# Attention scores on one core: four heads side by side in 64x32 PE tiles, with k read at a stride of 256 B

## Chip, core and metric

The kernel runs on one core of one Trainium2 chip. The metric is the device time of one launch in microseconds. Three runs of the kernel before took 211.76, 212.16 and 212.25 us, so the median is 212.16 us.

## What is computed

```python
def setup_inputs():
    batch, heads, seq, dim = 8, 8, 512, 64
    ...
def reference(q, k):
    scale = 1.0 / np.sqrt(q.shape[-1])
    return (np.einsum('bhqd,bhkd->bhqk', q, k) * scale).astype(np.float32)
```

There are 64 products, one for each batch and head. Each multiplies a 512x64 q by a transposed 512x64 k and gives a 512x512 float32 matrix. The inputs are 16.8 MB, the output is 67.1 MB.

## The kernel before

The kernel is written with a tile library: it declares pools of buffers and operations, and a scheduler orders the instructions of each engine and puts in the waits.

**Loading.** `load(b)` reads the whole q and k of a batch (8 heads) into `qf` and `kf`, 128 partitions by 8 heads by 4 rows of 64 floats (lines L49 and L50). Partition p holds rows 4p to 4p+3 of every head, so a head's piece in one partition is 4x64x4 B = 1 KB of contiguous memory. Batch 0 is loaded in four pieces of two heads each, the others in one piece of 1 MB for q and one for k. `raw_pool` has three buffers. Batches 0 and 1 are requested at the start, batch b+2 in the middle of batch b. All transfers, loads and stores, are issued by SP, in one queue.

**Per pair of heads** (`g`, four per batch) GpSimd casts the q and the k of two heads to bf16 (L81; ScalarE and VectorE do it for the first pair). TensorE transposes them in eight 128x128 steps into PSUM (`tq`, `tk`, L89). ScalarE copies `tq` to `qT` (L92). VectorE copies `tk` to `kT` (L93) and reorders on the way: it writes the elements with a stride of four, so that the columns of k lie in their natural order and the matmul can read them contiguously. After the transpose the first head of the pair lies on partitions 0 to 63 and the second on 64 to 127.

**Matmuls.** For each of the four row groups of q there is one matmul for each head (L101): 64 rows deep, 128 columns of weights (`qT`), 512 columns of k streamed. The tile position puts the two heads in the two row halves of the array. Two row groups fill one `ps` buffer of a head (128 x 1024 floats, two PSUM banks). There are three such buffers. `evacuate` scales a full `ps` buffer into the output tile `o`, alternately on ScalarE (L63) and VectorE (L65).

**Storing.** One store for each pair of heads (L108) moves the 2 MB tile `o`: in each partition two pieces of 8 KB, one per head. `out_pool` has seven buffers of 16 KB per partition.

Of the kernel before, what the change touches and what calls it, by code (L numbers as in the profile page):

```python
# [1 line left out]

# [5 lines left out]


@with_exitstack  # L10
def kernel(
    ctx: ExitStack,
    tc: tile.TileContext,
    q: bass.AP,
    k: bass.AP,
    out: bass.AP,
):


    nc = tc.nc  # L20
    B, H, S, D = q.shape
    scale = 1.0 / (D ** 0.5)
    P = 128
    J = S // P
    PAIRS = H // 2

    f32 = mybir.dt.float32
    bf16 = mybir.dt.bfloat16

    q_r = q.rearrange("b h (p j) d -> b p h (j d)", j=J)  # L30
    k_r = k.rearrange("b h (p j) d -> b p h (j d)", j=J)
    out_r = out.rearrange("b h (p j) k -> b p h (j k)", j=J)

    consts = ctx.enter_context(tc.tile_pool(name="consts", bufs=1))
    raw_pool = ctx.enter_context(tc.tile_pool(name="raw", bufs=3))
    bf_pool = ctx.enter_context(tc.tile_pool(name="bf", bufs=3))
    t_pool = ctx.enter_context(tc.tile_pool(name="t", bufs=3))
    out_pool = ctx.enter_context(tc.tile_pool(name="out", bufs=7))
    tpsum_pool = ctx.enter_context(tc.tile_pool(name="tpsum", bufs=1, space=bass.MemoryType.PSUM))
    psum_pool = ctx.enter_context(tc.tile_pool(name="psum", bufs=3, space=bass.MemoryType.PSUM))  # L40

    raws = {}

    def load(b):
        qf = raw_pool.tile([P, H, J * D], f32, name="qf")
        kf = raw_pool.tile([P, H, J * D], f32, name="kf")
        step = 2 if b == 0 else H
        for h in range(0, H, step):
            nc.sync.dma_start(out=qf[:, h:h + step, :], in_=q_r[b, :, h:h + step, :])  # L49
            nc.sync.dma_start(out=kf[:, h:h + step, :], in_=k_r[b, :, h:h + step, :])  # L50
        raws[b] = (qf, kf)

    load(0)
    identity = consts.tile([P, P], dtype=bf16)
    make_identity(nc, identity)
    load(1)

    n_evac = 0

    def evacuate(dst, src):  # L60
        nonlocal n_evac
        if n_evac % 2 == 0:
            nc.scalar.mul(out=dst, in_=src, mul=scale)  # L63
        else:
            nc.vector.tensor_scalar(out=dst, in0=src, scalar1=scale, scalar2=None,  # L65
                                    op0=mybir.AluOpType.mult)
        n_evac += 1

    for b in range(B):
        qf, kf = raws.pop(b)  # L70
        for g in range(PAIRS):
            if g == PAIRS // 2 and b + 2 < B:
                load(b + 2)
            qb = bf_pool.tile([P, J, 2, D], bf16, name="qb")
            kb = bf_pool.tile([P, J, 2, D], bf16, name="kb")
            first = b == 0 and g == 0
            for slab, dst, copy in (
                (qf, qb, nc.scalar.copy if first else nc.gpsimd.tensor_copy),
                (kf, kb, nc.vector.tensor_copy if first else nc.gpsimd.tensor_copy),
            ):  # L80
                copy(out=dst.rearrange("p j h d -> p h j d"),  # L81
                     in_=slab[:, 2 * g:2 * g + 2, :].rearrange("p h (j d) -> p h j d", j=J))
            qT = t_pool.tile([P, J, P], bf16, name="qT")
            kT = t_pool.tile([P, P, J], bf16, name="kT")
            tq = tpsum_pool.tile([P, J, P], bf16, name="tq")
            tk = tpsum_pool.tile([P, J, P], bf16, name="tk")
            for slab, tp in ((qb, tq), (kb, tk)):
                for j in range(J):
                    nc.tensor.transpose(out=tp[:, j, :],  # L89
                                        in_=slab[:, j].rearrange("p h d -> p (h d)"),  # L90
                                        identity=identity)
            nc.scalar.copy(out=qT, in_=tq)  # L92
            nc.vector.tensor_copy(out=kT.rearrange("d p j -> d j p"), in_=tk)  # L93

            o = out_pool.tile([P, 2, J * S], f32, name="o")
            for i in range(0, J, 2):
                pss = [psum_pool.tile([P, 2, S], f32, name="ps") for _ in range(2)]
                for u in range(2):
                    for h in range(2):
                        rows = slice(h * D, (h + 1) * D)  # L100
                        nc.tensor.matmul(out=pss[h][:, u, :], lhsT=qT[rows, i + u, :],  # L101
                                         rhs=kT[rows].rearrange("d p j -> d (p j)"),
                                         start=True, stop=True,
                                         tile_position=(h * D, 0))
                for h in range(2):
                    evacuate(o[:, h, i * S:(i + 2) * S],
                             pss[h].rearrange("p u k -> p (u k)"))
            nc.sync.dma_start(out=out_r[b, :, 2 * g:2 * g + 2, :], in_=o)  # L108


# [1 line left out]
_INS = ['q', 'k']  # L112
_OUTS = [((8, 8, 512, 512), 'float32')]


# [23 lines left out]
```

## Time and profile before

| | |
|---|---|
| median of three runs | 212.16 us |
| the profiled execution | 212.47 us |
| its span on the core | 210.7 us |
| PE matmul busy | 123.5 us (59%), 512 instructions |
| PE weight load busy | 40.5 us (19%), 512 instructions |
| VectorE / ScalarE / GpSimd busy | 115.3 / 84.7 / 36.9 us |
| moved by DMA | 83.99 MB, mean 399 GB/s |
| store of one `o`: issue to landing | 19.3 us, median |

The span is the time between the first and the last instruction on the core in one profiled execution; the 1.77 us beside it lie around it. The profile gives busy time for each engine, the share of the 16 DMA engines that was busy in each slice of the span, groups of equal instructions with their mean duration, and for every wait which instruction ended it. A transfer's "landing" is the moment at which its semaphore is complete. A store is issued as soon as its tile is full, and then stands in line behind the transfers issued before it.

### The profile page before, as it was taken

The numbers are of one execution on the slowest core, as the hardware profiler recorded it, in microseconds if no ns is written. First come the engines' busy times: TensorE is split into PE (matmuls) and PEld (weight loads), VectorE is DVE, ScalarE is ACT, GpSimd is POOL, SyncE is SP. The second block draws the span as 40 slices with busy tenths as digits, with TensorE's granted clock in tenths as the row PEclk, the third lists the DMA queues.
The fourth block names the chain that finished last, engine by engine and source line by source line (L and its number), as shares of the span: only waits on it lengthen the run. The fifth ranks groups of instructions, "written<-read, shape, count | busy, mean of one in ns | idle before, by whom it ended". The sixth has DMA issues, their size and how long they took to land.

```text
span 210.7 us, 1559 instructions
## 1 busy us (share of the span) xinstructions
PE 123.5 (59%) x512; PEld 40.5 (19%) x512; DVE 115.3 (55%) x97; ACT 84.7 (40%) x98; POOL 36.9 (18%) x68
## 2 busy tenths in 40 slices
PE   1899999897778743886148870587705877000000
PEld 0323222322232102221032210422104221000000
DVE  0699989688748940688307872178712797100000
ACT  4456666565536432446134460345503555000000
POOL 1625213300530006200070000800008000000000
DMA  6999999999999999999999999999999999999990
GB/s 185 335 357 411 428 403 425 429 426 394 401 428 425 426 382 413 428 425 423 376 425 429 426 412 386 426 431 428 398 400 426 428 428 426 428 426 428 431 409 37
DMA packets 25448, 83.99 MB, mean 399 GB/s; under 512 B 864, under 2 KB 17248, under 8 KB 17248
## 3 DMA queue, kind: packets, MB, share of 16 engines
q1 hardware_dynamic: 25440, 83.89, 99.1%
q8 instruction: 4, 0.07, 0.1%
q14 instruction: 4, 0.03, 0.0%
HBM read 16.78 MB, written 67.11 MB: 398 GB/s over the span
## 4 chain that ended last, share of the span: by engine, by line
DMA 50%; PE 8%; DVE 6%; ACT 1%; issue 0%; POOL 0%; DVEq 0%
DMA kf<-in_k_dram 50%; PE ps L101 6%; DVE kT L93 4%; DVE o L65 2%; PE tk L89 2%; ACT o L63 1%; POOL kb L81 0%; PE tq L89 0%; DVEq L65 0%
## 5 line engine op out<-in xcount | busy, mean ns | idle before, releaser
L101 PE MATMUL ps<-kT,qT 64*128 64x512 bf16 x256 | 90.1, 615 | 15.5 <-DVE o L65 5.9
L65 DVE TENSOR_SCALAR o<-ps 128x1024 f32<-128x1024 f32 x64 | 78.1, 1228 | 20.1 <-PE ps L101 18.7
L63 ACT ACTIVATE o<-ps 128x1024 f32<-128x1024 f32 x64 | 64.2, 1022 | 47.9 <-PE ps L101 47.8
L93 DVE COPY kT<-tk 128x512 bf16<-128x512 bf16 x32 | 41.3, 1291 | 39.7 <-PE tk L89 39.1
L89 PE MATMUL tq<-identity,qb 128*128 128x128 bf16 x128 | 21.6, 303 | 36.5 <-POOL qb L81 23.2
L81 POOL CAST qb<-qf 128x512 bf16<-128x512 f32 x31 | 18.2, 613 | 117.5 <-DMA qf<-in_q_dram 103.0
L92 ACT COPY qT<-tq 128x512 bf16<-128x512 bf16 x32 | 18.7, 585 | 43.5 <-PE tq L89 40.7
L101 PEld LDWEIGHTS <-qT 64*128 64x128 bf16 x256 | 16.2, 111 | 56.8 <-issue 55.9
L89 PEld LDWEIGHTS <-qb 128*128 128x128 bf16 x128 | 12.9, 131 | 56.3 <-POOL qb L81 29.6
L89 PE MATMUL tk<-identity,kb 128*128 128x128 bf16 x128 | 19.5, 307 | 3.0 <-DVE kT L93 2.5
L81 POOL CAST kb<-kf 128x512 bf16<-128x512 f32 x31 | 18.3, 613 | 7.9 <-DMA kf<-in_k_dram 3.7
L89 PEld LDWEIGHTS <-kb 128*128 128x128 bf16 x128 | 12.2, 134 | 24.0 <-issue 19.1
L81 DVE CAST kb<-kf 128x512 bf16<-128x512 f32 x1 | 0.4, 427 | 4.7 <-DMA kf<-in_k_dram 4.7
L81 ACT ACT_TABLE_LOAD x1 | 1.3, 1283 | 0.7 <-PEq L123 0.7
L81 ACT CAST qb<-qf 128x512 bf16<-128x512 f32 x1 | 0.6, 617 | 1.4 <-DMA qf<-in_q_dram 1.4
masks.py:199 POOL TENSOR_SCALAR_AFFINE_SELECT identity<-identity 128x128 bf16<-128x128 bf16 x1 | 0.3, 292 | 0.1
masks.py:197 POOL MEMSET identity<- 128x128 bf16 x1 | 0.2, 204 | 0.3 <-POOLq L123 0.3
L123 POOL MEMSET const-float32-0.0<- 128x1 f32 x1 | 0.1, 98 | 0.2 <-issue 0.2
L123 POOL MEMSET const-bfloat16-1.0<- 128x1 bf16 x1 | 0.1, 101 | 0.0
L123 POOL MEMSET const-uint8-127<- 128x1 uint8 x1 | 0.1, 101 | 0.0
L123 POOL MEMSET const-float32-1.0<- 128x1 f32 x1 | 0.1, 98 | 0.0
## 6 DMA issues: line engine op xcount, KB each, us to landing
out_dram<-o SPq DMA_DIRECT2D x32, 2048.0 KB, 19.3
qf<-in_q_dram SPq DMA_DIRECT2D x7, 1024.0 KB, 26.0
kf<-in_k_dram SPq DMA_DIRECT2D x7, 1024.0 KB, 27.5
qf<-in_q_dram SPq DMA_DIRECT2D x4, 256.0 KB, 4.3
kf<-in_k_dram SPq DMA_DIRECT2D x4, 256.0 KB, 4.6
```

The costliest lines, as they stand in the source:

```text
L63: nc.scalar.mul(out=dst, in_=src, mul=scale)
L65: nc.vector.tensor_scalar(out=dst, in0=src, scalar1=scale, scalar2=None, op0=mybir.AluOpType.mult)
L81: copy(out=dst.rearrange("p j h d -> p h j d"), in_=slab[:, 2 * g:2 * g + 2, :].rearrange("p h (j d) -> p h j d", j=J))
L89: nc.tensor.transpose(out=tp[:, j, :], in_=slab[:, j].rearrange("p h d -> p (h d)"), identity=identity)
L92: nc.scalar.copy(out=qT, in_=tq)
L93: nc.vector.tensor_copy(out=kT.rearrange("d p j -> d j p"), in_=tk)
L101: nc.tensor.matmul(out=pss[h][:, u, :], lhsT=qT[rows, i + u, :], rhs=kT[rows].rearrange("d p j -> d (p j)"), start=True, stop=True, tile_p ...
L123: nc = _bacc.Bacc("TRN2", target_bir_lowering=False, num_devices=1)
```

## The change

The tiling of heads and rows changes. Eight heads become 2 (`x`) times 4 (`g`), and 128 partitions become 4 heads (`g`) times 32 groups of rows (`m`), each with 16 consecutive rows (`j`, R = 16).

- A partition now holds 16 rows of one head: 4 KB contiguous for each load piece, two pieces (`x`) per partition. k is requested before q, and batch 0 comes whole like the others.
- GpSimd does all casts, in 128x1024 pieces, four per batch.
- The transposes take 128 partitions by 64 columns: 64 per batch (2 operands, 16 `j`, 2 `x`), 512 in all, in place of 256 of 128x128. `x` selects partitions 0 to 63 or 64 to 127 of the result. Eight `j` share one PSUM buffer `tp` (two buffers).
- `kT` is copied as it lies, with `j` outside and partitions inside. The order of the columns of k is restored by the matmul's read: for each head `g` it walks over `m` outside and `j` inside, and a step of `j` is 128 bf16 elements, 256 B.
- A matmul is 64 rows deep with 32 columns of weights (one head's 32 row groups at one `j`) and 512 streamed columns. Eight such tiles, 2 row halves by 4 column groups, cover the array. There are 1024 in place of 256.
- An output tile `o` holds one `x`, four heads and 8 consecutive rows in each partition: 16 KB contiguous in a partition and in memory. Each half batch has two such tiles and two stores of 2 MB. `out_pool` has six buffers instead of seven; `bf`, `t` two instead of three.

```diff
-    q_r = q.rearrange("b h (p j) d -> b p h (j d)", j=J)
-    k_r = k.rearrange("b h (p j) d -> b p h (j d)", j=J)
-    out_r = out.rearrange("b h (p j) k -> b p h (j k)", j=J)
+    q_r = q.rearrange("b (x g) (m j) d -> b (g m) x (j d)", x=2, j=R)
+    k_r = k.rearrange("b (x g) (m j) d -> b (g m) x (j d)", x=2, j=R)
+    out_r = out.rearrange("b (x g) (m j) k -> b x (g m) j k", x=2, j=R)
...
-        for h in range(0, H, step):
-            nc.sync.dma_start(out=qf[:, h:h + step, :], in_=q_r[b, :, h:h + step, :])
-            nc.sync.dma_start(out=kf[:, h:h + step, :], in_=k_r[b, :, h:h + step, :])
+        nc.sync.dma_start(out=kf, in_=k_r[b])
+        nc.sync.dma_start(out=qf, in_=q_r[b])
...
+        for x in range(2):
+            for slab, dst in ((kf, kb), (qf, qb)):
+                nc.gpsimd.tensor_copy(out=dst[:, x].rearrange("p j d -> p (j d)"), in_=slab[:, x])
...
+        for slab in (kb, qb):
+            for j0 in range(0, R, JB):
+                tp = tpsum_pool.tile([P, JB, P], bf16, name="tp")
+                for j in range(JB):
+                    for x in range(2):
+                        nc.tensor.transpose(out=tp[x * D:(x + 1) * D, j, :],
+                                            in_=slab[:, x, j0 + j, :], identity=identity)
+                if slab is kb:
+                    nc.vector.tensor_copy(out=kT[:, j0:j0 + JB, :], in_=tp)
+                else:
+                    nc.scalar.copy(out=qT[:, j0:j0 + JB, :], in_=tp)
...
+        kTg = kT.rearrange("d j (g m) -> d g m j", g=G)
+        for j0 in range(0, R, JB):
+            os = [out_pool.tile([P, JB, S], f32, name="o") for _ in range(2)]
+            for j in range(0, JB, 2):
                 pss = [psum_pool.tile([P, 2, S], f32, name="ps") for _ in range(2)]
                 for u in range(2):
-                    for h in range(2):
-                        rows = slice(h * D, (h + 1) * D)
-                        nc.tensor.matmul(out=pss[h][:, u, :], lhsT=qT[rows, i + u, :],
-                                         rhs=kT[rows].rearrange("d p j -> d (p j)"),
-                                         start=True, stop=True,
-                                         tile_position=(h * D, 0))
+                    for g in range(G):
+                        cols = slice(g * M, (g + 1) * M)
+                        for x in range(2):
+                            rows = slice(x * D, (x + 1) * D)
+                            nc.tensor.matmul(out=pss[x][cols, u, :],
+                                             lhsT=qT[rows, j0 + j + u, cols],
+                                             rhs=kTg[rows, g, :],
+                                             start=True, stop=True,
+                                             tile_position=(x * D, g * M))
+                for x in range(2):
+                    evacuate(os[x][:, j:j + 2, :], pss[x])
+            for x in range(2):
+                nc.sync.dma_start(out=out_r[b, x, :, j0:j0 + JB, :], in_=os[x])
+            if j0 == 0 and b + 2 < B:
+                load(b + 2)
```

The scheduler decides where the requests stand in SP's queue. In the program that it builds from the changed kernel, SP first issues the loads of batches 0, 1 and 2 and of batch 3's k, then the stores from the first one on; batch 3's q comes behind the sixth store.

More of the change, by code (lines that the diff above doesn't have):

```diff
@@ L23 @@
     P = 128
-    J = S // P
-    PAIRS = H // 2
+    G = H // 2
+    M = P // G
+    R = S // M
+    JB = 8
     f32 = mybir.dt.float32
     bf16 = mybir.dt.bfloat16
-    q_r = q.rearrange("b h (p j) d -> b p h (j d)", j=J)
-    k_r = k.rearrange("b h (p j) d -> b p h (j d)", j=J)
-    out_r = out.rearrange("b h (p j) k -> b p h (j k)", j=J)
+    q_r = q.rearrange("b (x g) (m j) d -> b (g m) x (j d)", x=2, j=R)
+    k_r = k.rearrange("b (x g) (m j) d -> b (g m) x (j d)", x=2, j=R)
+    out_r = out.rearrange("b (x g) (m j) k -> b x (g m) j k", x=2, j=R)
     consts = ctx.enter_context(tc.tile_pool(name="consts", bufs=1))
     raw_pool = ctx.enter_context(tc.tile_pool(name="raw", bufs=3))
[L36 to L39, printed above, removed]
+    bf_pool = ctx.enter_context(tc.tile_pool(name="bf", bufs=2))
+    t_pool = ctx.enter_context(tc.tile_pool(name="t", bufs=2))
+    out_pool = ctx.enter_context(tc.tile_pool(name="out", bufs=6))
+    tpsum_pool = ctx.enter_context(tc.tile_pool(name="tpsum", bufs=2, space=bass.MemoryType.PSUM))
     psum_pool = ctx.enter_context(tc.tile_pool(name="psum", bufs=3, space=bass.MemoryType.PSUM))
@@ L44, in load @@
     def load(b):
-        qf = raw_pool.tile([P, H, J * D], f32, name="qf")
-        kf = raw_pool.tile([P, H, J * D], f32, name="kf")
-        step = 2 if b == 0 else H
-        for h in range(0, H, step):
-            nc.sync.dma_start(out=qf[:, h:h + step, :], in_=q_r[b, :, h:h + step, :])
-            nc.sync.dma_start(out=kf[:, h:h + step, :], in_=k_r[b, :, h:h + step, :])
+        qf = raw_pool.tile([P, 2, R * D], f32, name="qf")
+        kf = raw_pool.tile([P, 2, R * D], f32, name="kf")
+        nc.sync.dma_start(out=kf, in_=k_r[b])
+        nc.sync.dma_start(out=qf, in_=q_r[b])
         raws[b] = (qf, kf)
@@ L70 @@
         qf, kf = raws.pop(b)
[L71 to L96, printed above, removed]
@@ new lines @@
+        qb = bf_pool.tile([P, 2, R, D], bf16, name="qb")
+        kb = bf_pool.tile([P, 2, R, D], bf16, name="kb")
+        for x in range(2):
+            for slab, dst in ((kf, kb), (qf, qb)):
+                nc.gpsimd.tensor_copy(out=dst[:, x].rearrange("p j d -> p (j d)"), in_=slab[:, x])
+        qT = t_pool.tile([P, R, P], bf16, name="qT")
+        kT = t_pool.tile([P, R, P], bf16, name="kT")
+        for slab in (kb, qb):
[9 more added lines that the diff above has]
+                    nc.scalar.copy(out=qT[:, j0:j0 + JB, :], in_=tp)
@@ L105 @@
[L105 to L108, printed above, removed]
+                    for g in range(G):
[7 more added lines that the diff above has]
+                                             tile_position=(x * D, g * M))
```

## The prediction

> **What bounds the kernel now.** I read the busy line first, then the DMA rows, then the tail, then the PE timeline.
>
> ```profile
> PE 123.5 (59%) x512; PEld 40.5 (19%) x512; DVE 115.3 (55%) x97; ACT 84.7 (40%) x98; POOL 36.9 (18%) x68
> DMA  6999999999999999999999999999999999999990
> ...
> q1 hardware_dynamic: 25440, 83.89, 99.1%
> q8 instruction: 4, 0.07, 0.1%
> ...
> DMA 50%; PE 8%; DVE 6%; ACT 1%; issue 0%; POOL 0%; DVEq 0%
> ```
>
> No engine is busy for over 59% of the span, while the DMA row is full from the second slice to the last but one. The kernel is bound by its transfers. The busy time in stretches says at what rate, and how it ends:
>
> ```profile
> 8.00:11.00 3.00, 3.00 (x14) 1.04 (x11) 2.58 (x3) 1.94 (x2) 1.84 (x3) 1.00 1.04 350
> ...
> 190.00:200.00 10.00, 0.00 (x0) 0.00 (x0) 0.00 (x0) 0.00 (x0) 0.00 (x0) 1.00 1.01 429
> ...
> 206.00:207.00 1.00, 0.00 (x0) 0.00 (x0) 0.00 (x0) 0.00 (x0) 0.00 (x0) 1.00 0.16 66
> 207.00:208.00 1.00, 0.00 (x0) 0.00 (x0) 0.00 (x0) 0.00 (x0) 0.00 (x0) 1.00 0.06 25
> 208.00:209.00 1.00, 0.00 (x0) 0.00 (x0) 0.00 (x0) 0.00 (x0) 0.00 (x0) 1.00 0.06 25
> ```
>
> The last two numbers are the DMA engines' share and GB/s. Before the first store (12.2 us) only loads run, in 1 KB pieces: 350 GB/s. From 180 us on only stores run, in 8 KB pieces: 426 to 429. After 206.2 us a share of 0.06, one engine of 16, works on until 209.4: it lags by 3.2 us. The q8 row names a candidate: four instruction fetches of 16 KB, which I take to be for PE, whose 1026 rows of the program at 64 B would make 66 KB.
>
> The stores take 67.1 MB / 427.5 = 157.0 us. The transfers run from 1.9 to 206.2 us, so 47.3 us are left for 16.8 MB of loads: 355 GB/s, as the load-only stretch shows. The span is then 1.9 + 47.3 + 157.0 + 3.2 (lag) + 1.3 (from 209.4 to the end) = 210.7.
>
> The timeline gives PE's rates. Two matmuls of different row halves take 0.61 us together, two pairs 1.03:
>
> ```profile
> 45.06 0.61 PE L101 MATMUL ps<-kT,qT 64*128 64x512 bf16 x2 [0.42 <-DVE kT L93]
> ```
> ```profile
> 45.06 1.03 PE L101 MATMUL ps<-kT,qT 64*128 64x512 bf16 x4 [0.42 <-DVE kT L93]
> 46.03 0.61 PE L89 MATMUL tk<-identity,kb 128*128 128x128 bf16 x4
> ```
>
> A pass of 512 columns costs 0.42 us and about 0.19 us of latency once; a transpose costs (0.61 - 0.29) / 3 = 0.107 us.
>
> **What the Trainium skill says.** "TensorE: Matmul & The Clock Gate", Back-to-back issue gap, gives N / 1.2 ns for a cold array: 427 ns for 512 and 107 for 128 columns. The trace agrees with both, so the array runs at that rate although the granted clock is shown as 1.00. Its Part 3 reports small tiles in row and column groups running at once, 16 of them at 10.6 times one; the trace shows row halves together (0.61 above), no column groups. "SBUF — State Buffer", Door 1, says that an access needs two hits on a 16-byte line for full bandwidth. The new read of k hits every line once, with no such matmul in this trace. "DMA: Bandwidth & Descriptors", iDMA fabric, has a load stream of 4 KiB rows at 408.7 GB/s; the trace has only 1 KB loads.
>
> **The change part by part.**
>
> *Loads*, 4 KB pieces: 16.78 MB / 408.7 = 41.1 us, 6.2 less. A line through 1 KB at 355 and 8 KB at 427.5 GB/s gives 415 (40.4 us) as the better end; 47.3 is the worse. *Stores*, 16 KB pieces: I leave 157.0; that line gives 434 GB/s, so 2.4 us less is the better end, and a loss by the new 32 KB pitch of the partitions in memory isn't excluded but has nothing for it.
>
> *Instruction fetch.* The built program has 3074 PE rows for 1026. Three times four fetches at 3.2 / 4 = 0.8 us (0.62, two 8 KB pieces at one engine's 26.7 GB/s, at the low end) is 9.6 (7.4) us on the lagging engine; I take 8.4, so 5.2 more.
>
> Sum before any idle DMA: 1.9 + 41.1 + 157.0 + 8.4 + 1.3 = **209.7**.
>
> *The start* decides how long DMA idles. Before, 256 KB pieces let the first store go at 12.2 us. Now k of batch 0 (1 MB) lands at 1.9 + 2.6 + 0.85 (what the first 256 KB load took beyond its transfer) = 5.3, q at 7.9. POOL casts in the order k0, q0, k1, q1, each twice the 613 ns of L81: ends 6.5, 9.1, 10.3, 11.5. k's transposes need both halves: from 10.3. A batch has 64 transposes; with half the columns each costs 0.107 if serial, 0.053 if two column halves run at once; I take 0.08. k's 32 end at 12.9, q's at 15.4. ACT's copy of qT's first half (1.1 us, twice the 585 ns of L92) ends by 15.5, DVE's copies of kT (1.2, the price of L65) earlier. Matmuls start at 15.6.
>
> *The matmuls.* The eight tiles do not run side by side as the words say: in the built program the scheduler puts all eight matmuls of one `ps` buffer together, four column groups, then the same four at the next row, all in one row half. One buffer is two passes; the next buffer, in the other half, can overlap one. The pass is the unknown. Its ends: 0.427 us, as contiguous; 1.71, if the four column groups, which read the same partitions, share one line a cycle. A faster array (0.213) would gain at most 2 us at the start. The nearest row is L93's copy, which writes 2-byte elements 8 B apart: 1291 ns, against 585 for the contiguous copy of the same size (L92). That is 2.2 times, and the skill's two hits say the same, so I take **0.854**.
>
> The first store needs four buffers of each half: three buffers, 14 transposes of the next batch, three buffers, 6 transposes, a buffer, 7 transposes, a buffer. From 15.6: three at one pass each plus one, to 19.0; 20.1; 23.5; 24.0; the seventh is full at 25.9 and evicted (1.02) at 26.95, the eighth follows at 29.4. First bytes leave at 28.05. The seven loads queued ahead (7.34 MB) end at 19.9. DMA idles **8.2 us**.
>
> *After that* a half batch costs 8 buffers of max(0.854, (2 x 0.854 + 0.19 + 1.25) / 3 = 1.05) us, for three buffers and an eviction, or 1.2 where transposes break the overlap, and 32 x 0.08: 12.2 us. Its two stores take 9.8, with loads 12.4. Until loads come between the stores (behind the sixth) two half batches are late by 2.4 us: **4** in round. Later production, about 23 to 24.6 us a batch, just keeps up with DMA's 24.7.
>
> *At nothing:* DVE's 41.3 us of kT copies become 16 of about 1.2; no gain, as DVE has 45% idle. POOL casts the same bytes under DMA. Batch 3's k load waits on SP for the third cast (10.3), with the stores behind it; none is due before 26. Six `o` buffers for seven still queue 12 MB, 29 us of stores; if production fell behind, that cover is gone.
>
> Span 209.7 + 8.2 + 4 = 221.9; about 1 us of fetches falls into idle time: 221. Beside the span lie 1.77 us, and the profiled execution was 0.31 above the median: **222.4**.
>
> **The rivals.**
>
> *A strided pass costs nothing* (0.427). For it: the array takes a column only every 0.83 ns, and may need no second hit. The same chain gives the first store at 22.75, first bytes 23.85, 4 us idle, then no more: 213.7, in time **214.5** (209 to 217). The fetches and the late start eat the gain of the loads.
>
> *Faster.* One mechanism, the larger pieces, decides if the lag doesn't grow: fetches spread over engines (3.2 stays), loads at 415, stores at 434, a free stride with paired transposes (2 us idle). 1.9 + 40.4 + 154.6 + 3.2 + 1.3 + 2 = 203.4, **204.9**. It turns when lag and idle time together grow by less than what the pieces save (6.2 to 9.3 us). Against it: one engine's tail is in the trace.
>
> *PE becomes the bound.* Four column groups share one line a cycle: pass 1.71, a batch 16 x 1.71 + 64 x 0.08 + 1 = 33.5 us, eight 268, plus 10.3 ahead and 13 for the last evictions and stores: 291, **293**. For it: the four reads hit the same partitions at once.
>
> **How the numbers follow.** Stride at twice: 0.38. Free stride: 0.30. Faster: 0.13. PE-bound: 0.17, and 0.02 for the rest. The likeliest alone covers 216 to 240 (transposes 0.053 to 0.107, production just behind DMA). The range 204.5 to 242 takes in all but the PE-bound case and the edges. A measurement here can tell about 0.3%. Faster 0.13; same 0.06, out of the free stride; slower 0.81.
>
> **What would show it.** Loads alone at 400 to 415 GB/s; DMA empty from about 20 to 28 us; 12 q8 fetches and a one-engine tail of some 8 us; two passes of a `ps` in about 1.9 us. Wrong if the DMA row stays full at the start, if one `ps` takes 1.0 us, or if PE is busy throughout and the DMA row has gaps in every batch.

## The result, and the profile after

The changed kernel takes 233.55 us (median of four runs, 233.04 to 234.31) against 211.97 us before in the same comparison: 1.102 times, with an interval of 1.0986 to 1.1054. The prediction had the sign, but 10.2 us of loss where there are 21.6. The profiled execution has a span of 231.7 us, 21.0 more than before.

The head of the page, its DMA queues and its chain of waits:

```profile
PE 191.9 (83%) x1536; PEld 45.9 (20%) x1536; DVE 88.6 (38%) x80; ACT 82.1 (35%) x81; POOL 33.1 (14%) x38
PE   0289999999998989898898988898998989989700
PEclk9995667796575555566555555557555555557555
DMA  6995494979989999999999999999999998909896
...
q1 hardware_dynamic: 8960, 83.89, 89.2%
q8 instruction: 12, 0.20, 0.3%
...
PE 77%; ACT 8%; DVE 5%; DMA 3%; POOL 1%; issue 1%; SPq 0%
PE ps L103 69%; PE tp L86 7%; ACT o L65 6%; DMA qf<-in_q_dram 3%; ACT qT L91 3%; DVE o L67 3%; DVE kT L89 2%; POOL qb L77 0%; POOL kb L77 0%; SPq L51 0%
```

The bound has moved. PE rose from 123.5 to 191.9 us of busy time, and the chain, half of which was DMA, now runs through PE for 77%, 69% in the matmuls. DMA has dips: at the start, then small ones, and one at 200 us (DMA share 0.38 from 200 to 210 us).

The groups of the matmul and of VectorE's copy of k, then the stretches of the start (busy times and numbers of instructions of PE, PEld, DVE, ACT and POOL, then clock, DMA share and GB/s):

```profile
L103 PE MATMUL ps<-kT,qT 64*32 64x512 bf16 x1024 | 161.3, 1026 | 15.5 <-ACT o L65 13.5
...
L89 DVE COPY kT<-tp 128x1024 bf16<-128x1024 bf16 x16 | 11.0, 686 | 16.4 <-PE tp L86 16.3
```
```profile
18.00:20.00 2.00, 2.00 (x33) 1.10 (x33) 0.00 (x0) 1.03 (x1) 1.44 (x3) 0.50 1.03 408
20.00:22.00 2.00, 2.00 (x16) 0.13 (x4) 1.13 (x1) 0.00 (x0) 0.81 (x1) 0.50 0.21 84
22.00:24.00 2.00, 2.00 (x18) 0.43 (x14) 1.46 (x3) 1.02 (x1) 0.00 (x0) 0.50 0.00 0
24.00:26.00 2.00, 2.00 (x19) 0.60 (x23) 0.46 (x1) 1.03 (x1) 0.00 (x0) 0.50 0.00 0
26.00:28.00 2.00, 2.00 (x24) 0.31 (x11) 0.76 (x1) 0.00 (x0) 0.00 (x0) 0.75 0.67 287
```

A single matmul takes 1026 ns where the kernel before had 615. DMA is all but empty from about 20.6 to 26.6 us: the loads queued ahead are done, and the first store is issued at 25.91.

The steady state is in the chain of waits. This is one full turn of it (start, duration, what; steps of "issue" below 0.05 us are left out):

```profile
123.71 9.85 PE ps L103 x62
133.59 1.03 ACT o L65
134.66 3.63 PE ps L103 x24
138.31 1.23 DVE o L67
139.54 0.60 DVE kT L89
140.15 0.70 DVE kT L89
140.90 1.08 PE tp L86 x16
142.00 1.02 ACT qT L91
143.06 6.66 PE ps L103 x39
149.74 1.03 ACT o L65
150.81 9.86 PE ps L103 x64
```

From 123.71 to 150.81 is 27.1 us, and the next batches repeat it (177.91, 205.00). The three matmul stretches hold 8, 3 and 5 `ps` buffers and take 9.85 + 3.63 + 6.66 = 20.1 us. Twice PE stands still while ScalarE evicts a buffer, 1.1 us each. Between 138.29 and 143.06 lie the transposes and the copies of `kT` and `qT`, 4.8 us.

DMA would need less for a batch: 2.1 MB of loads at 418 GB/s (the stretch from 8 to 12 us) and 8.4 MB of stores at 431 (e4 below) are 24.5 us. Little room is left, as its share over a turn (143.06 to 170.17 us) is 0.98. But PE waits for no transfer in that turn: its waits are 2.2 us for ScalarE's evictions, 0.5 for `qT` and 0.4 for `kT`. So DMA is fed too slowly by PE, and nothing that the larger transfers save is left.

At a standstill only one of the three `ps` buffers is full. These are the evictions that lead up to the first one:

```profile
130.57 1.03 ACT L65 ACTIVATE o<-ps 128x1024 f32<-128x1024 f32 x1 [0.75 <-PE ps L103]
131.81 1.23 DVE L67 TENSOR_SCALAR o<-ps 128x1024 f32<-128x1024 f32 x1 [1.50 <-PE ps L103]
133.59 1.02 ACT L65 ACTIVATE o<-ps 128x1024 f32<-128x1024 f32 x1 [1.98 <-PE ps L103]
134.66 3.60 PE L103 MATMUL ps<-kT,qT 64*32 64x512 bf16 x24 [1.12 <-ACT o L65]
```

Two buffers are free from 131.60 and 133.04 us on, yet PE waits for the third, which it has only just filled. At 149.72 us it is the same.

Not all batches take 27.1 us. The four that begin at 88.87, 115.97, 143.06 and 170.17 do. The three before them took 74.4 us, from the first matmul at 14.50 to 88.87, 24.8 us each on average. There the chain has transposes of the next batch between the matmul stretches, and only two standstills:

```profile
14.50 3.61 PE ps L103 x23
18.11 0.89 PE tp L86 x12
19.00 3.53 PE ps L103 x24
22.53 0.46 PE tp L86 x6
```

### The profile page after: what moved, and what is told of

It is laid out like the page before. It is cut to its first block, busy times and chain, and to the rows that moved or that the text cites. A ratio compares the mean times of both kernels' runs of the same rounds, so it can differ in the third digit from the quotient of the medians.

```text
span 231.7 us, 3444 instructions
## 1 busy us (share of the span) xinstructions
PE 191.9 (83%) x1536; PEld 45.9 (20%) x1536; DVE 88.6 (38%) x80; ACT 82.1 (35%) x81; POOL 33.1 (14%) x38
## 4 chain that ended last, share of the span: by engine, by line
PE 77%; ACT 8%; DVE 5%; DMA 3%; POOL 1%; issue 1%; SPq 0%
PE ps L103 69%; PE tp L86 7%; ACT o L65 6%; DMA qf<-in_q_dram 3%; ACT qT L91 3%; DVE o L67 3%; DVE kT L89 2%; POOL qb L77 0%; POOL kb L77 0%; SPq L51 0%
## 5 line engine op out<-in xcount | busy, mean ns | idle before, releaser
L103 PE MATMUL ps<-kT,qT 64*32 64x512 bf16 x1024 | 161.3, 1026 | 15.5 <-ACT o L65 13.5
L65 ACT ACTIVATE o<-ps 128x1024 f32<-128x1024 f32 x64 | 65.7, 1026 | 105.9 <-PE ps L103 99.9
L103 PEld LDWEIGHTS <-qT 64*32 64x32 bf16 x1024 | 19.1, 104 | 119.3 <-issue 114.4
L77 POOL CAST kb<-kf 128x1024 bf16<-128x1024 f32 x16 | 16.3, 1043 | 100.6 <-DMA kf<-in_k_dram 70.0
L91 ACT COPY qT<-tp 128x1024 bf16<-128x1024 bf16 x16 | 15.6, 1013 | 30.2 <-PE tp L86 30.2
L86 PE MATMUL tp<-identity,kb 128*64 128x128 bf16 x256 | 17.5, 305 | 10.1 <-POOL kb L77 10.1
L77 POOL CAST qb<-qf 128x1024 bf16<-128x1024 f32 x16 | 16.3, 1043 | 41.7 <-DMA qf<-in_q_dram 41.6
L86 PEld LDWEIGHTS <-kb 128*64 128x64 bf16 x256 | 13.3, 162 | 39.1 <-issue 27.1
L86 PE MATMUL tp<-identity,qb 128*64 128x128 bf16 x256 | 16.2, 296 | 2.1 <-DVE kT L89 1.8
L89 DVE COPY kT<-tp 128x1024 bf16<-128x1024 bf16 x16 | 11.0, 686 | 16.4 <-PE tp L86 16.3
L86 PEld LDWEIGHTS <-qb 128*64 128x64 bf16 x256 | 14.0, 160 | 13.5 <-issue 13.5
```

The costliest lines, as they stand in the source:

```text
L77: nc.gpsimd.tensor_copy(out=dst[:, x].rearrange("p j d -> p (j d)"), in_=slab[:, x])
L86: nc.tensor.transpose(out=tp[x * D:(x + 1) * D, j, :], in_=slab[:, x, j0 + j, :], identity=identity)
L89: nc.vector.tensor_copy(out=kT[:, j0:j0 + JB, :], in_=tp)
L91: nc.scalar.copy(out=qT[:, j0:j0 + JB, :], in_=tp)
L103: nc.tensor.matmul(out=pss[x][cols, u, :], lhsT=qT[rows, j0 + j + u, cols], rhs=kTg[rows, g, :], start=True, stop=True, tile_position=(x * ...
```

## The experiments

Two theories. **S**: the stride. Every element of the strided read lies on a new 16-byte line (the line is the Trainium skill's, "SBUF — State Buffer", Door 1), and costs two column times. A "hit" below is one element read from such a line. **C**: the column groups. Four 32-column tiles that stream at once share what one tile had. Beside them the question why a batch took 27.1 us when the prediction, with the pass of theory S, had about 23 to 24.6.

### e3: the stride alone, in the kernel before

```diff
-            kT = t_pool.tile([P, P, J], bf16, name="kT")
+            kT = t_pool.tile([P, J, P], bf16, name="kT")
...
-            nc.vector.tensor_copy(out=kT.rearrange("d p j -> d j p"), in_=tk)
+            nc.vector.tensor_copy(out=kT, in_=tk)
...
-                                         rhs=kT[rows].rearrange("d p j -> d (p j)"),
+                                         rhs=kT[rows].rearrange("d j p -> d p j"),
```

> The kernel before, with one edit: kT is copied as it lies and the matmul (64x128 tiles, no column groups) reads k's columns at a stride of 256 B. Theory S: a pass takes 0.85 us without any column groups, four matmuls of two row halves about 1.9 us in place of 1.03, PE needs 5.7 to 6.5 us for each pair of heads where a 2 MB store with its loads needs 6.2: 212 to 228 us. Theory C: the pass stays at 0.43 us and the time at 212 us. VectorE's k copies fall from 1.29 to about 0.4 us under both.

Measured: 221.71 us, 1.0452 times the kernel before (1.0425 to 1.0479). The matmul group, and VectorE's copy of k:

```profile
L101 PE MATMUL ps<-kT,qT 64*128 64x512 bf16 x256 | 161.3, 1030 | 0.5 <-DVE kT L93 0.5
...
L93 DVE COPY kT<-tk 128x512 bf16<-128x512 bf16 x32 | 13.5, 423 | 38.2 <-PE tk L89 38.2
```

The mean of a matmul goes from 615 to 1030 ns, the same as in the changed kernel, with no column group in the program. The difference, 415 ns, is about one more pass of 512 columns (0.42 us in the kernel before). VectorE saves 0.87 us in each copy and nobody gains by it.

### e1: the column groups without the stride

```diff
-        kT = t_pool.tile([P, R, P], bf16, name="kT")
+        kT = t_pool.tile([P, P, R], bf16, name="kT")
...
-                    nc.vector.tensor_copy(out=kT[:, j0:j0 + JB, :], in_=tp)
+                    nc.vector.tensor_copy(out=kT[:, :, j0:j0 + JB].rearrange("d p j -> d j p"), in_=tp)
...
-        kTg = kT.rearrange("d j (g m) -> d g m j", g=G)
+        kTg = kT.rearrange("d (g m) j -> d g (m j)", g=G)
```

> The changed kernel, but VectorE's copy puts k's columns back into natural order (2-byte writes at a stride of 32 B), so that the matmul streams them contiguously; tiles, loads and stores as in the changed kernel. Theory S (each read of a new 16-byte line takes two column times): a pass falls from 0.85 to 0.43 us, eight matmuls of a ps buffer from 1.9 to 1.04 us, PE is no longer the bound, the DMA row fills again after a late first store: span 213 to 215, time about 215 us. Theory C (four column groups share the streaming, the stride is innocent): a pass stays at 0.85 us and the time at 231 us or more. VectorE's k copies rise from 0.69 to about 2.5 us each under both.

Measured: 221.65 us, 1.0462 times before (1.0433 to 1.0492).

```profile
L103 PE MATMUL ps<-kT,qT 64*32 64x512 bf16 x1024 | 92.9, 596 | 25.6 <-ACT o L65 18.7
L65 ACT ACTIVATE o<-ps 128x1024 f32<-128x1024 f32 x64 | 64.7, 1023 | 57.9 <-PE ps L103 54.3
L89 DVE COPY kT<-tp 128x1024 bf16<-128x1024 bf16 x16 | 70.7, 4558 | 11.4 <-PE tp L86 11.4
```

The mean of 596 ns is a mixture. The matmuls from 57.5 to 63.9 us, where the clock row shows 1.00, and those from 64.0 to 84.4, where it shows 0.50:

```profile
L103 PE MATMUL ps<-kT,qT 64*32 64x512 bf16 x72 | 4.8, 380 | 0.7 <-ACT o L65 0.5
L103 PE MATMUL ps<-kT,qT 64*32 64x512 bf16 x108 | 10.6, 616 | 8.4 <-DVE o L67 5.5 <-ACT o L65 2.5 <-ACT qT L91 0.4
```

On PE theory S is confirmed and C excluded: 64x32 tiles with four column groups take 616 ns with a contiguous read, as the kernel before had, and eight matmuls of one `ps` buffer 1.04 us.

For some microseconds the array was faster still: 380 ns a matmul, and 226 ns a transpose in place of 313 (30 to 57 us). The strided read gains nothing from that state. In the changed kernel from 27.1 to 30.2 us the transposes are as short (219 to 227 ns), and the strided matmuls take 1029:

```profile
L103 PE MATMUL ps<-kT,qT 64*32 64x512 bf16 x24 | 4.6, 1029 | 0.0
L86 PE MATMUL tp<-identity,kb 128*64 128x128 bf16 x6 | 0.4, 227 | 0.0
```

So "twice" holds against the slower array, at which the kernel before ran throughout.

The time missed my expectation (215), because the stride has to go somewhere: VectorE's copy, which now writes 2 bytes every 32, takes 4.56 us instead of 0.69. I had 2.5. VectorE's `kT` copy is now the first line of the chain (29%).

### e2: two hits on a line

```diff
-        kT = t_pool.tile([P, R, P], bf16, name="kT")
+        kT = t_pool.tile([P, R // 2, P, 2], bf16, name="kT")
...
-                    nc.vector.tensor_copy(out=kT[:, j0:j0 + JB, :], in_=tp)
+                    nc.vector.tensor_copy(out=kT[:, j0 // 2:(j0 + JB) // 2].rearrange("d a p c -> d a c p"),
+                                          in_=tp.rearrange("d (a c) p -> d a c p", c=2))
...
-        kTg = kT.rearrange("d j (g m) -> d g m j", g=G)
+        kTg = kT.rearrange("d a (g m) c -> d g m a c", g=G)
```

> The changed kernel with kT laid out so that rows j and j+1 of a group are neighbours: the matmul reads two bf16 (4 B) from a 16-byte line, then steps 512 B. If two hits on a line are enough (theory S as the Trainium skill words it): a pass of 0.43 us, time as with contiguous reads, about 214 us, with a cheaper VectorE copy. If every change of line costs one extra column time: three times for two columns, a pass of 0.64 us, time 218 to 224. Theory C: 0.85 us and 231 us.

Measured: 213.92 us, 1.0084 times before (1.0058 to 1.0111).

```profile
L104 PE MATMUL ps<-kT,qT 64*32 64x512 bf16 x1024 | 122.8, 707 | 19.3 <-ACT o L65 15.4
...
L89 DVE COPY kT<-tp 128x1024 bf16<-128x1024 bf16 x16 | 21.0, 1351 | 13.4 <-PE tp L86 13.4
```

The time is the one expected for two hits being enough, the mean of a matmul is not quite: 707 ns lies above e1's 616, so a pass is about 0.09 us longer than a contiguous one on the slower array, a fifth of the single hit's penalty. From 16.4 to 64.0 us the array was in its faster state (224 ns a transpose), and the matmuls still took 705 ns where e1's contiguous ones took 380. The Trainium skill, "SBUF — State Buffer", Door 1, asks for at least two hits on a line for full bandwidth. In this run two were nearly enough for the slower array, and not enough for the faster one. DMA is the bound again (its share is 1.01 from 60 to 180 us), but still idles at the start: 76 GB/s from 20 to 22 us.

### e6: smaller eviction units, stride kept

```diff
-    psum_pool = ctx.enter_context(tc.tile_pool(name="psum", bufs=3, space=bass.MemoryType.PSUM))
+    psum_pool = ctx.enter_context(tc.tile_pool(name="psum", bufs=6, space=bass.MemoryType.PSUM))
...
-                pss = [psum_pool.tile([P, 2, S], f32, name="ps") for _ in range(2)]
+                pss = [psum_pool.tile([P, S], f32, name="ps") for _ in range(2)]
```

> The changed kernel with its strided read, but six ps buffers of one PSUM bank (128x512) in place of three of two banks, each evicted by itself. Theory ring (the 2.4 us a batch by which PE was later than the prediction come from buffers of two passes that wait for one another's eviction, and not from the passes): PE's idle time before matmuls goes, a batch takes 19 to 24 us of PE time, below DMA's 24.7, the DMA row fills after the start and the time is 216 to 221 us, although a pass still takes 0.85 us. Rival: the passes themselves are the bound, since the two row halves do not overlap: 32 passes of 0.85 are 27 us a batch and the time stays at 230 us or more. VectorE's evictions become 128 of about 0.69 us, 23.6 us a batch with its k copies, close to the bound.

Measured: 216.15 us, 1.0174 times before (1.0143 to 1.0206), 17.4 us less than the changed kernel.

```profile
L102 PE MATMUL ps<-kT,qT 64*32 64x512 bf16 x1024 | 141.7, 1021 | 16.6 <-ACT o L65 12.3
L67 DVE TENSOR_SCALAR o<-ps 128x512 f32<-128x512 f32 x128 | 87.9, 691 | 79.4 <-PE ps L102 79.4
L65 ACT ACTIVATE o<-ps 128x512 f32<-128x512 f32 x128 | 76.7, 600 | 78.4 <-PE ps L102 76.3
```

The first matmuls of batches 0 and 1:

```profile
14.28 11.47 PE L102 MATMUL ps<-kT,qT 64*32 64x512 bf16 x104 [0.48 <-ACT qT L91]
32.35 1.90 PE L102 MATMUL ps<-kT,qT 64*32 64x512 bf16 x16 [0.51 <-ACT qT L91]
```

The single matmul is as slow as in the changed kernel (1021 ns), and yet most of the loss is gone. At the start the two row halves now do run side by side: 104 matmuls take 11.47 us from 14.28 us on, eight in 0.88. The second batch's matmuls start at 32.35 us, 18.1 after the first's, where the changed kernel took 23.8 (14.50 to 38.31). Later a batch takes 24.1 us (matmuls start at 129.35 and 153.48), about DMA's 24.5, and the DMA share is 1.01 from 100 to 180 us. Of the 3.0 us by which this turn is shorter, 2.0 are in the matmul stretches (18.1 in place of 20.1).

So the stride doubles the pass, but it costs the kernel most of its time only together with buffers of two such passes. Either change takes most of the loss away: the shorter pass of e2 with the old buffers, or the smaller buffers here with the long pass. This edit changes the size of the buffers, their number and with them the order of the waits, all at once.

### e4 and e5: the transfers alone

e4 has the changed kernel's loads and stores, e5 those of the kernel before, in their sizes and in the order of the program text; everything between is left out and the stores send zeros. With no computation to wait for, the first stores go out early (at 4.4 us in e4), so these runs price the transfers and not the start.

> The transfers of the changed kernel alone, in its sizes, order and queue: no casts, transposes, matmuls or evictions, the stores send tiles that were filled with zeros once. If the larger pieces are worth what the prediction says: loads at 409 to 415 GB/s, stores at 427 to 434, span 198 to 202 us. If the lag of one DMA engine comes from PE's instruction fetches, it is gone here: no tail of a single engine beyond 1 us, no q8 row. If the larger pieces are worth nothing, the span equals that of the other transfers-only kernel.

> The transfers of the kernel before alone, likewise without any computation: 1 KB load pieces, 8 KB store pieces. The prediction's sum without the lag: 1.9 + 47.3 + 157.0 + 1.3 = 207.5 us of span, 6 to 9 more than with the changed kernel's pieces, and no tail of one engine.

Measured: e4 204.98 us, 0.9638 times before (0.9604 to 0.9672), span 202.3; e5 210.27 us, 0.9901 times (0.9866 to 0.9936), span 207.6. The two spans are those of the fastest of four executions; the medians of the spans are 203.2 and 208.3. The prediction's sum without fetches was 207.5 for e5's transfers and 201.3 for e4's. The larger pieces are worth 5.3 us. Neither profile has a q8 row, the queue of the instruction fetches.

### e9: instruction fetches

```diff
+    for n in range(1536):
+        nc.tensor.matmul(out=pt, lhsT=w, rhs=w[:, :64], start=True, stop=True)
```

The kernel is e4 with these matmuls beside it; w is constant.

> The transfers-only kernel with the changed kernel's pieces, and beside it 1536 matmuls of 64 columns on constant data, which read nothing that is loaded and which nothing waits for: PE's 3072 instruction rows without their work. If instruction fetches make one DMA engine late: about twelve q8 fetches, a tail of a single engine of 7 to 10 us, span 209 to 212 us against 202.3 without the matmuls. If the lag before had another cause: span 202 to 203 us.

Measured: 207.83 us, 0.9787 times before (0.9764 to 0.981), span 205.9. The queue, and a stretch near the end:

```profile
q8 instruction: 12, 0.20, 0.3%
```
```profile
202.00:203.00 1.00, 0.00 (x0) 0.00 (x0) 0.00 (x0) 0.00 (x0) 0.50 0.08 33
```

PE's instructions alone, without work for anyone, lengthen the time by 2.9 us (e4 204.98; the two profiled spans differ by 3.6) and bring back the tail, in which about one engine of 16 is busy. So the mechanism fits, though the run does not separate the fetches from PE's mere running. The size was overstated: 0.24 us for each of twelve fetches, where I had 0.7. I had divided the whole lag before (3.2 us) by the four fetches on the q8 row. That page has four more on q14, and leaving out all computation (e5) gains only 2.0 us of time.

### e7, e8 and e10: towards a faster kernel

e7 is e2 with the two transposes of a row joined into one of 128x128 and the first batch loaded in four pieces that VectorE and ScalarE cast. e8 also cuts the first half batch's stores:

```diff
                 for x in range(2):
                     evacuate(os[x][:, j:j + 2, :], pss[x])
+                    if b == 0 and j0 == 0:
+                        nc.sync.dma_start(out=out_r[b, x, :, j:j + 2, :], in_=os[x][:, j:j + 2, :])
```

e10 is built like e8, but takes two heads side by side instead of four.

```diff
-    G = H // 2
+    G = 2
+    X = H // G
```

> The changed kernel with k's rows read in neighbouring pairs (4 B a line), the two transposes of a row joined into one of 128x128 (256 in place of 512), and the first batch loaded in four pieces of 512 KB, cast by VectorE and ScalarE. First store before the loads queued ahead end at 20 us, so DMA does not idle at the start; two instruction fetches fewer; span 203 to 207 us, time 205 to 209 us, below the kernel before. If DMA still idles at the start, or if the one-engine tail stays at over 5 us, 210 us or more.

> The kernel with pairs, joined transposes and split first loads, and the stores of the first half batch cut into eight of 512 KB, each issued as soon as its ps buffer is evicted. In the run without this cut DMA was empty from 18.5 to 21.4 us, while the first two tiles of 2 MB filled. If that gap is what is left of the start, it goes: 2.5 to 3 us less, time 210 to 211 us. If something else starves DMA there (a wait of SP on earlier transfers, a later shortage in the second batch), the time stays at 213 us.

> A middle way: two heads side by side in 64x64 tiles, 8 rows of each head in a partition (load pieces of 2 KB, store pieces of 16 KB), 512 matmuls, 256 joined transposes, so 1538 PE rows in place of 3074; k read in pairs of 4 B; batch 0 loaded in halves, its first half stored in eight pieces. Loads of 2 KB at about 390 GB/s (between 355 and the changed kernel's rate): 43 us; stores 156; five or six fetches, 4 us; no idle time at the start: span 205 to 208 us, time 206.5 to 209.5 us, below the kernel before. If PE's passes of about 0.5 us bind, or if DMA idles at the start, 211 us or more.

Measured: e7 213.39 us, 1.0039 times before (1.0021 to 1.0057), a miss; DMA was empty around 20 us, as the first 2 MB tiles were full only at 20.9. e8 210.16 us, **0.9918** (0.9887 to 0.9949): a small gain on the kernel before, under 1%, and far below the changed kernel. e10 210.49 us, 0.9922 (0.9893 to 0.9950), no better with half the changed kernel's PE instructions. Its loads of 2 KB and its short first stores move 374 GB/s from 10 to 20 us, e8's 414; that this is why it gains nothing was not tested. e8's DMA row has no gap:

```profile
DMA  6999999999999999999999999999999999999981
...
q8 instruction: 10, 0.16, 0.3%
```

Of the 5.3 us that the pieces are worth without computation, 2.1 arrive (212.23 to 210.16).

## Why the prediction was right or wrong

**Right, its size by luck: the pass.** In the changed kernel two passes and their latency take 1.88 us, so a pass is about 0.85; e1 and e3 show that it comes from the stride and not from the column groups. The two ends of the bound, a free stride and one shared line for four groups, are both excluded. The factor behind the predicted 0.854 compared VectorE's strided copy (1291 ns) with ScalarE's contiguous one (585, L92). VectorE's own contiguous copy of that size takes 423 ns (e3), a factor of 3.1, which would have made the pass 1.3 us. That a ratio of two engines' copies came near the matmul's two was luck.

**Right: the transfers.** Loads run at 417 to 419 GB/s between 4 and 12 us (408.7 predicted), and the spans of e5, 207.6 to 208.6 us, lie within 1.1 us of the prediction's sum.

**Right: the start.** First matmuls at 14.50 (15.6 predicted), first store at 25.91 (26.95), DMA empty for about 6 us (8.2). The three small misses go one way: a transpose cost 0.05 to 0.06 us instead of 0.08, a cast 1.04 instead of 1.23, the `kT` copy 0.69 instead of 1.2.

**Wrong: "8 buffers of max(0.854, ... = 1.05) us, for three buffers and an eviction, or 1.2 where transposes break the overlap".** This term was mis-sized, and with it the sentence that production "just keeps up with DMA's 24.7". (With 64 transposes of 0.08 us the two sizes make 21.9 to 24.3 us a batch, not the "23 to 24.6" stated.) The first three batches, 24.8 us each, came close to it. In the four that follow, the 16 buffers of a batch take 20.1 us of matmul stretches and 2.2 of standing still, 22.3 / 16 = 1.39 us each; the transposes and copies take 4.8, where the sum had 5.1. A batch is 27.1 us. The 2.6 us above DMA's 24.5 recur in each of these four, and this change from a transfer-bound to a PE-bound kernel is what the prediction missed. It had named the signs: PE busy throughout, and gaps in the DMA row. That 233.55 us lies inside its range of 204.5 to 242 is luck, for the range was drawn to leave out a PE-bound kernel.

My formula let three buffers turn in a ring, each half overlapping the other. The built program's waits come in runs instead, three buffers in a row after ScalarE's evictions and then two after VectorE's, and the trace shows the row halves one after the other in large part: 16 buffers at 0.85 us would be 13.7 us. e6 shows that the buffers are the cause, since it halves them, keeps the slow pass and brings the first batch from 23.8 to 18.1 us. At the two standstills of a turn the other two buffers are free, so what holds PE there is the order of the waits and not the depth of three. For the matmul stretches the two were not separated.

**Wrong, without consequence: the fetches.** 8.4 us should have been about 2.9 (e9). In the PE-bound kernel the term hardly shows in the result: the DMA share falls to 0.09 at 229.5 us and to nothing at 230.0, where the kernel before had a tail of 3.2 us. The right sum is made on PE's side: 14.5 us to the first matmul, 74.4 for three batches, 108.4 for four, and 23.5 from the last batch's first matmul (197.3) to the end of its last eviction (220.8). The last two stores and the end take the remaining 10.9 us.

**The rivals.** The faster one needed a free stride and no growth of the lag; the first is false. The PE-bound rival named the right bound by a wrong mechanism, four groups on one line, and so gave 293 us.

## What to carry to other kernels

A reordering that is moved from a copy into a matmul's read is not free: ask how many neighbouring elements are touched in a row, on the side that writes as well as on the side that reads, and look for a layout like e2's, where both sides stay cheap enough. When an operation becomes slower, work out the cycle of its buffers (fill, wait, evict, in the order of the built program) and not only the operation. Larger transfer pieces were worth 5.3 us here, and a late first store left DMA empty for about 6: cut the first stores small.

## What the hardware showed that I had not expected

- A matmul of 512 columns read at one element per line took 1030 ns with 64x128 tiles and 1026 ns with 64x32 tiles; with two neighbours per line 707 ns; contiguous 615 and 616 ns, and 380 ns in a stretch of e1 in which the array was faster. The strided and the paired read took no less in that state (1029 and 705 ns).
- VectorE's copy of 128x1024 bf16 out of PSUM takes 686 ns written contiguously, 1351 ns with 2-byte writes 4 B apart, 4558 ns 32 B apart.
- The PEclk row alone does not tell a contiguous matmul's speed. At 1.00 it took 615 ns in the kernel before, 616 in e1 from 30 to 57 us and 380 from 57.5 to 63.9; at 0.50 it took 616. The strided pass is the same at both: three buffers took 3.60 us at 18.93 us (clock 0.50) as at 25.30 us (0.50, then 0.75 to 1.00).
- Instruction fetches of 16 KB go with about one late DMA engine at the end of a transfer-bound kernel, 0.24 us per fetch in e9.
